# A two-layer S5, neighbourhood-attention and latent-attention block: the second layer's attention bias made in another stage, four gates moved to the first stage, the compressed projections cut in two jobs

## The chip, the cores and the metric

The kernel runs on one core of a Trainium2 chip. The metric is the device time of one execution in microseconds (us); lower is better. TensorE is PE in the rows (its weight loads PEld), VectorE is DVE, ScalarE is ACT, GpSimd is POOL, and SyncE, which here only issues transfers, is SP (SPq is its queue of transfers). Each engine, and each queue of transfers, runs its instructions in the order in which the program holds them.

## The reference

Two layers (`DEPTH = 2`) over 512 latent tokens (`x`) and 256 context tokens (`ctx`), 1024 channels, float32. Each layer feeds one modulated input `h` to three mixers and merges them:

```python
(ua, za, qn, kn, vn, zn, cq, ckv, kr, zm, ga, gn, gm) = split_cols(h @ w_in)
ya = s5_mixer(ua, ...)      # recurrence, then y = gelu(y); y * sigmoid(y @ w_glu + b_glu)
yn = neighbourhood_attention(qn, kn, vn, ..., rpb)     # bias from rpb, per layer
ym = block_attention(mla_queries(cq, ...), mla_keys_values(ckv, kr, ...))
m = (sig(ga) * ((ya * silu(za)) @ w_branch_a)
     + sig(gn) * ((yn * silu(zn)) @ w_branch_b)
     + sig(gm) * ((ym * silu(zm)) @ w_branch_c))
x = layer_norm(alpha * x + gate * (m @ w_out))
```

`cq`, `ckv` and `kr` are the compressed queries, keys and rotary keys (416 columns of `w_in`); `ga`, `gn` and `gm` are three gates of 1024 columns each; `rpb` is the table of the neighbourhood attention's bias. Only the latent tokens come out, so that the context's tokens go through the last half of layer 0 alone.

## The kernel before

Channels lie on the partitions and tokens along the free axis, 768 tokens (512 latent, 256 context). Every product is made in three passes: each operand is split into a rounded high part and the rest (`split`: ACT copies the high part, DVE or POOL subtracts), and PE multiplies high by high, low by high and high by low. A projection of 128 columns of `w_in` (`project`, matmuls at L232) is 24 matmuls of 512 tokens and 24 of 256 tokens; its weights are loaded as `wr` (four buffers), split into `wh` and `wl`. Low parts are `wl`, `hl`, `al` (line 145 on DVE or POOL), high parts `wh`, `hh`, `ah` (line 142 on ACT).

A layer has five stages, each with its own pools of SBUF. In the first (`s5a`) a string of letters, `JOBS[l]`, sets the order of the jobs: `u` makes the input of the recurrence, `a` and `m` the silu gates `za` and `zm` of two branches, `B` builds one of four sets of tables of the recurrence on DVE with small matmuls (L197, L659), `c` projects half of the compressed columns (three tiles of 128 tokens, matmuls at L1051), norms them, transposes them and stores them (`c_d`, `kr_d`), and `N` makes layer 0's bias table. Then come the neighbourhood attention and the recurrence (`na`), the latent attention (`mla`), the merge (`mrg`) and the output projection (`out`). In the profile layer 0's stages begin at about 0, 245, 478, 700 and 960 us, layer 1's at about 1085, 1200, 1390, 1570 and 1737.

The bias of layer `l` is made by `na_bias_layer`: for one or two heads three small loads from `rpb_d` fill 48 rows, POOL adds a mask, and one store writes `na_zd`. Layer 1's is made in layer 0's merge, in eight steps over four buffers of 480 columns.

The merge runs through branch b (8 blocks of 128 output channels), branch c (8 blocks, each with its gate `gm`), then the gates `ga` that are not yet made, then the S5 output's GLU (4 blocks of 24 matmuls), then branch a (8 blocks). `GX` says how many `ga` gates the latent attention makes in its spare room (two in layer 0, as gates 0 and 1; gates 2 to 7 are left to the merge). Work beside the blocks is placed by a string with a letter for each block:

```python
SIDE = ('T....B.B..N...G.........', '................G.......')
```

Position 0 is block 0 of branch b, position 8 block 0 of branch c: `T` and `B` make layer 1's tables, `N` its bias, `G` the gelu, which loads `y` (two buffers), squares, tanh on ACT, products on POOL and DVE, and splits into `ah0` and `al0`. All transfers of this stage go through SP's queue.

`split` goes round the engines by a counter: from the end of layer 0's first stage on, `flip` counts the calls and a table says for each stage which call in how many goes to DVE (`SE_REST = (3, (0,))`, one in three, holds in layer 1's merge).

## Time and profile before

| | |
|---|---|
| three runs | 1785.62, 1791.37, 1793.07 us (median 1791.37) |
| the profiled execution | 1788.85 us |
| its span, first to last instruction | 1787.1 us |
| mean granted clock of TensorE | 0.973 of full speed (2.4 GHz) |
| busy: PE, DVE, ACT, POOL | 1655.7, 1238.3, 746.9, 379.7 us |
| share of the span | 93%, 69%, 42%, 21% |

The span is 1.75 us shorter than the profiled execution's own time; a sum of changes of the span is made against 1788.85 us, which lies 2.52 us under the median. The busy shares are means over ten stages; what an edit is worth is read in its own stage.

### The profile page before, as it was taken

Reading aid. Unit: us, or ns where it says so; the run is one execution under the profiler, and the core shown is the slowest. Engines: PE = TensorE matmul, PEld = TensorE weight load, DVE = VectorE, ACT = ScalarE, POOL = GpSimd, SP = SyncE. Lnnn points to the kernel's source line nnn. Section 1 sums busy time; section 2 is a strip of 40 time slices with the busy share of each in tenths; the row PEclk is TensorE's granted clock in tenths of the full one; section 3 lists DMA queues with packets and bytes.
Section 4 is the critical chain, followed back from the end, with each engine's and each line's share of the span. In section 5 each row is a group of like instructions: output and inputs, shape, how many; then the busy total and the mean of one; then the engine's idle time right before and its main releaser. Section 6 shows DMA issues by size and latency. Waiting matters only on the chain.

```text
span 1787.1 us, 29011 instructions
## 1 busy us (share of the span) xinstructions
PE 1655.7 (93%) x10808; PEld 1387.4 (78%) x10808; DVE 1238.3 (69%) x2722; ACT 746.9 (42%) x1466; POOL 379.7 (21%) x284
## 2 busy tenths in 40 slices
PE   4899699999989999999799988899999999999996
PEld 2687588888878888878688767788888888788865
DVE  4899948877746564989357688838888666762257
ACT  4423344335355565222243345442344555642241
POOL 2000111012221101201403542001111311245382
PEclk9899799999999999999899999999999999999999
DMA  9567785345321122655756726755554422253462
GB/s 307 158 191 222 207 248 153 94 143 141 84 78 56 58 69 97 232 164 170 192 167 219 189 90 192 225 162 164 156 165 120 126 76 65 83 154 106 130 206 71
DMA packets 273076, 264.87 MB, mean 148 GB/s; under 512 B 70440, under 2 KB 227896, under 8 KB 272936
## 3 DMA queue, kind: packets, MB, share of 16 engines
q1 hardware_dynamic: 271736, 259.93, 49.4%
q0 software_dynamic: 1200, 3.10, 0.5%
q8 instruction: 85, 1.39, 0.3%
q14 instruction: 55, 0.45, 0.1%
HBM read 198.64 MB, written 68.53 MB: 149 GB/s over the span
## 4 chain that ended last, share of the span: by engine, by line
PE 59%; DVE 13%; DMA 6%; ACT 3%; issue 2%; POOL 2%; SPq 1%; DVEq 0%; ACTq 0%; POOLq 0%
PE g L232 35%; PE s L197 5%; PE w L1375 4%; PE s L1403 3%; PE g L1608 2%; DVE sb L145 2%; PE w L1174 2%; PE s L1213 2%; PE w L719 1%; DVE wl L145 1%; DVE ln_rs L148 1%; DMA y<-y_d 1%; DMA wr<-in_w_out 1%; POOL macc L145 1%; PE w L758 1%
## 5 line engine op out<-in xcount | busy, mean ns | idle before, releaser
L232 PE MATMUL g<-hh,wh 128*128 128x512 f32 (+1 forms) x1344 | 479.3, 358 | 16.3 <-ACT wh L142 11.9
L232 PE MATMUL g<-hl,wh 128*128 128x512 f32 (+1 forms) x1344 | 477.0, 355 | 2.7 <-POOL hl L145 1.5
L232 PE MATMUL g<-hh,wl 128*128 128x512 f32 (+1 forms) x1344 | 475.9, 355 | 1.1 <-DVE wl L145 1.1
L232 PEld LDWEIGHTS g<-hh,wh 128*128 128x128 f32 x1344 | 256.3, 191 | 55.9 <-ACT wh L142 12.8
L232 PEld LDWEIGHTS g<-hl,wh 128*128 128x128 f32 x1344 | 256.4, 191 | 37.7 <-DVE hl L148 2.5
L232 PEld LDWEIGHTS g<-hh,wl 128*128 128x128 f32 x1344 | 255.9, 190 | 36.9 <-DVE wl L145 2.8
L142 ACT ACTIVATE wh<-wr 128x1024 fp32r<-128x1024 f32 (+1 forms) x150 | 155.2, 1036 | 227.4 <-PE g L232 139.8
L145 DVE TENSOR_TENSOR wl<-wr,wh 128x1024 fp32r<-128x1024 f32 (+1 forms) x118 | 153.6, 1305 | 114.0 <-ACT wh L142 113.3
L232 PE MATMUL g<-al,wh 128*128 128x512 f32 (+1 forms) x336 | 120.4, 359 | 1.8 <-DVE al L145 1.8
L232 PE MATMUL g<-ah,wl 128*128 128x512 f32 (+1 forms) x336 | 118.7, 358 | 1.2 <-POOL wl L145 1.1
L232 PE MATMUL g<-ah,wh 128*128 128x512 f32 (+1 forms) x336 | 119.7, 361 | 0.0
L145 POOL TENSOR_TENSOR wl<-wr,wh 128x1024 fp32r<-128x1024 f32 (+1 forms) x32 | 74.9, 2339 | 201.7 <-ACT wh L142 183.9
L142 ACT ACTIVATE mla_pt<-s 128x384 f32<-128x384 f32 (+1 forms) x128 | 59.4, 475 | 86.5 <-PE s L197 85.9
L1377 DVE TENSOR_REDUCE mla_sm<-w 128x1 f32<-128x768 f32 (+1 forms) x80 | 67.9, 849 | 34.2 <-PE w L1375 33.3
L145 POOL TENSOR_TENSOR macc<-macc,g_t 128x768 f32<-128x768 f32 (+1 forms) x32 | 56.5, 1769 | 146.3 <-DVE g_t L148 146.3
L232 PEld LDWEIGHTS g<-ah,wh 128*128 128x128 f32 x336 | 63.4, 189 | 14.4 <-issue 3.1
L142 ACT ACTIVATE na_p<-w,na_sm 128x512 f32<-128x512 f32 (+1 forms) x80 | 50.8, 643 | 54.6 <-DVE na_sm L152 48.3
L232 PEld LDWEIGHTS g<-al,wh 128*128 128x128 f32 x336 | 63.9, 190 | 12.3 <-DVE al L145 2.5
L232 PEld LDWEIGHTS g<-ah,wl 128*128 128x128 f32 x336 | 63.9, 190 | 11.6 <-POOL wl L145 2.5
L1608 PE MATMUL g<-woh,hh 128*128 128x512 f32 (+1 forms) x168 | 64.9, 386 | 4.3 <-ACT woh L142 4.2
L142 ACT ACTIVATE mla_p<-w,mla_sm 128x768 f32<-128x768 f32 (+1 forms) x80 | 65.0, 813 | 4.7 <-DVE mla_sm L152 4.5
L1608 PE MATMUL g<-woh,hl 128*128 128x512 f32 (+1 forms) x168 | 64.5, 384 | 0.0
(350 smaller groups left out, 3417.5 us busy)
## 6 DMA issues: line engine op xcount, KB each, us to landing
wr<-in_w_in SPq DMA_DIRECT2D x104, 512.0 KB, 4.6
wr<-in_w_mod SPq DMA_DIRECT2D x32, 512.0 KB, 4.6
s_w<-s_w SPq DMA_DIRECT2D x32, 512.0 KB, 4.3
s_o<-s_o SPq DMA_DIRECT2D x16, 568.0 KB, 5.8
wr<-in_w_out SPq DMA_DIRECT2D x16, 512.0 KB, 3.6
s_o<-sb SPq DMA_DIRECT2D x12, 576.0 KB, 4.4
wr<-in_w_in SPq DMA_DIRECT2D x16, 416.0 KB, 4.6
s_rc<-s_r SPq DMA_DIRECT2D x16, 384.0 KB, 3.2
```

The costliest lines, as they stand in the source:

```text
L142: return S.activation(out=o, in_=i, func=f, **kw)
L145: return e.tensor_tensor(out=o, in0=x, in1=y, op=op)
L148: V.scalar_tensor_tensor(out=o, in0=x, scalar=s, in1=y, op0=op0, op1=op1)
L197: PE.transpose(o, i, ident[:n, :n])
L232: PE.matmul(o, w[:, k], x[:, k, 0:n], start=(k == 0 and i == 0), stop=(k == nk - 1 and i == 2))
L719: PE.matmul(pv[64 * e:64 * e + 64, r, g // 2], w[:, g, 64 * r:64 * r + 64], u[:, g, 32 * d:32 * d + 96], start=True, stop=True)
L1174: PE.matmul(q[:, e, c:c + 256], qs[:, e, cq], k_[:, e, w0:w0 + 256], start=(j == 0), stop=(j == 1))
L1213: PE.matmul(po[64 * e:64 * e + 64, 0:128], v_t[:, t, 64 * e:64 * e + 64], pt[:, e, n], start=(n == 0), stop=(n == len(kt) - 1))
L1375: PE.matmul(q[:, c], x[0:96, cq], y[0:96, c], start=(j == 0), stop=(j == 2))
L1377: V.tensor_reduce(out=sm[:, 3:4], in_=q[:, k0:TOK], axis=AX.X, op=ALU.max)
L1403: PE.matmul(po[64 * e_:64 * e_ + 64, 0:128], v_t[:, t, 128 * i + 64 * e_:128 * i + 64 * e_ + 64], p2[e_][:, n], start=(n == 0), stop=(n == ...
L1608: PE.matmul(o, x[:, k, tok], w[k][:, c], start=(k == 0 and i == 0), stop=(k == 7 and i == 2))
```

## The change

Three edits, in the tables of letters and in three functions.

First, layer 1's bias leaves the merge (the `N` of `SIDE[0]`) and is made in layer 0's latent attention: `na_bias_layer` becomes a generator, one step (three loads, one add, one store) each time it is advanced, over the two buffers `g_t` that the gates of that stage use. Second, a new job `g` makes four `ga` gates in layer 0's first stage, so the latent attention's two are gates 4 and 5 and the merge has gates 6 and 7 left. Third, `c` stops after the norm and POOL's copies; the transposes, roundings and stores of the half are a job `k` of their own. `G` keeps its position 14 in `SIDE[0]`; what stands between it and the GLU gets shorter by four gates.

```diff
-SIDE = ('T....B.B..N...G.........', '................G.......')
+SIDE = ('T....B.B......G.........', '................G.......')
-JOBS = ('uuBaBmaBmBacmaNmc', 'maaBmmaBcamucuuu')
+JOBS = ('uuBaBmaBmBgacgkmgaNcgmk', 'maaBmmaBcakmucuuku')
...
             tt(P, z, z, mk.unsqueeze(1).to_broadcast([48, 15 * nh, 32]), ALU.add)
             Q.dma_start(out=zd[:, h:h + nh], in_=z.rearrange("p (h r) c -> p h (r c)", h=nh))
-        return zd
+            yield
+        zds.append(zd)
...
+                    yield
                     for i in (3, 2, 0, 1):
...
+                def compress(half):
+                    started.append(compressed(half))
+                    next(started[-1])
+
+                def compress_end(half):
+                    next(started[half], None)
+
+                def gate_s5(b):
+
+                    z = T(sa, [128, TOK], "z", 2)
+                    for s, n, o in project(C_GA + 128 * b, need_ctx):
+                        act(z[:, s], o, AF.Tanh, scale=0.5)
+                    ga[b] = T(dr, [128, TOK], f"ga_d{l}{b}")
+                    Q.dma_start(out=ga[b][:, 0:n_tok], in_=z[:, 0:n_tok])
+                    mod_step()
...
+                bias = na_bias_layer(l + 1, pds[0], mp, "g_t", 2, 640) if need_ctx else iter(())
...
                     if i < 3:
                         gate_n(2 * i + 2)
+                        next(bias, None)
                         gate_n(2 * i + 3)
+                    for _ in range(2 if i < 3 else 9):
+                        next(bias, None)
                     for _ in range(GX[l][i]):
                         gate_s(len(ga))
...
-                def next_bias():
-                    zds.append(na_bias_layer(l + 1, pds[0], side["b"], "sb", SB[1], 480))
```

How the instructions move shows in three places. On PE, the end of layer 0's first stage before: the last matmuls of the second compressed half (L1051), and behind them at once the query projection of the next stage (`g_2703`).

```order
L1051 MATMUL s_2296<-wh_2371,hh1_610 128x416
L1051 MATMUL s_2296<-wl_2372,hh1_610 128x416
L1051 MATMUL s_2296<-wh_2371,hl1_611 128x416
L232 MATMUL g_2703<-hh0_608,wh_2699 128x512
L232 MATMUL g_2703<-hl0_609,wh_2699 128x512
L232 MATMUL g_2732<-hh1_610,wh_2699 128x256
```

The same end of the second compressed half in the change: a gate's projection follows (`g_2554`, the fourth of the new gates).

```order
L1054 MATMUL s_2417<-wh_2492,hh1_610 128x416
L1054 MATMUL s_2417<-wl_2493,hh1_610 128x416
L1054 MATMUL s_2417<-wh_2492,hl1_611 128x416
L232 MATMUL g_2554<-hh0_608,wh_2550 128x512
L232 MATMUL g_2554<-hl0_609,wh_2550 128x512
L232 MATMUL g_2580<-hh1_610,wh_2550 128x256
```

The query projection (`g_2947`) now stands behind that gate, the last `m` gate (`g_2642` is its second part) and the second half's transposes of `ct`.

```order
L232 MATMUL g_2642<-hl1_611,wh_2611 128x256
L232 MATMUL g_2642<-hh1_610,wl_2612 128x256
L197 MATMUL s_2670<-ident_60,ct_2514 64x128 x3
L197 MATMUL s_2681<-ident_60,ct_2514 128x128 x3
L197 MATMUL s_2688<-ident_60,ct_2514 128x128 x3
L197 MATMUL s_2695<-ident_60,ct_2514 128x128 x3
L232 MATMUL g_2947<-hh0_608,wh_2943 128x512
```

On SP, in layer 0's merge, before: the tail of the 24 bias loads and 8 stores, among them the weights of the gates (`wr`, L215), and then the gelu's loads of `y`.

```order
L361 DMA sb_9095<-rpb_d_2204 16x15x32 x2
L215 DMA wr_9714<-in_w_in 128x8x128
L363 DMA na_zd1_9052<-sb_9089 48x480
L1517 DMA ga_d02_9711<-g_t_9652 128x768
L215 DMA wr_9775<-in_w_in 128x8x128
L215 DMA wr_9836<-in_w_in 128x8x128
L363 DMA na_zd1_9052<-sb_9095 48x480
L215 DMA wr_9897<-in_w_in 128x8x128
L215 DMA wr_9958<-in_w_in 128x8x128
L1470 DMA y_9497<-y_d00_95 128x768
L1470 DMA y_9515<-y_d01_96 128x768
```

The same place in the change: the weights of the two gates that are left are issued ahead of the tables' last transfers (`s5_k11`, `s5_w111`, `s5_t11`), and `y` follows these directly.

```order
L215 DMA wr_9897<-in_w_in 128x8x128
L215 DMA wr_9958<-in_w_in 128x8x128
L684 DMA s5_k11_8920<-s5_kds_8951 128x2x240
L683 DMA s5_w111_8914<-s5_w_9020 128x1024
L687 DMA s5_t11_8919<-s5_k11_8920 128x1x128 x8
L1493 DMA y_9741<-y_d00_95 128x768
L1493 DMA y_9759<-y_d01_96 128x768
L215 DMA wr_10020<-in_ssm_w_glu 128x4x256
```

On POOL, in layer 0's latent attention before, the splits of weights (`wl`, `uql`) and of queries (`mla_ql`) follow each other.

```order
L145 TENSOR_TENSOR mla_ql_5578<-mla_q_5555,mla_qh_5577 96x768
L145 TENSOR_TENSOR wl_6455<-wr_6452,wh_6454 128x1024
L145 TENSOR_TENSOR wl_6515<-wr_6512,wh_6514 128x1024
L145 TENSOR_TENSOR mla_ql_6089<-mla_q_6066,mla_qh_6088 96x768
L145 TENSOR_TENSOR uql_6596<-uqr_6590,uqh_6595 128x512
L145 TENSOR_TENSOR wl_6988<-wr_6985,wh_6987 128x1024
```

In the change one addition of the bias (`g_t`, 48 rows of 480) stands between nearly any two of them.

```order
L145 TENSOR_TENSOR mla_ql_5822<-mla_q_5799,mla_qh_5821 96x768
L145 TENSOR_TENSOR g_t_6221<-g_t_6221,na_mk_6218 48x480
L145 TENSOR_TENSOR wl_6720<-wr_6717,wh_6719 128x1024
L145 TENSOR_TENSOR g_t_6287<-g_t_6287,na_mk_6218 48x480
L145 TENSOR_TENSOR wl_6786<-wr_6783,wh_6785 128x1024
L145 TENSOR_TENSOR g_t_6293<-g_t_6293,na_mk_6218 48x480
L145 TENSOR_TENSOR mla_ql_6354<-mla_q_6331,mla_qh_6353 96x768
L145 TENSOR_TENSOR uql_6879<-uqr_6873,uqh_6878 128x512
L145 TENSOR_TENSOR g_t_6776<-g_t_6776,na_mk_6218 48x480
```

One thing moves without being written. The counter of `split` starts at the end of the first stage; four gates fewer are split after it, so the calls of layer 1's merge fall one place further on in the cycle of three. At that merge's end, of the eight splits of the merged sum (`hl`) three were on DVE and five on POOL, and now two and six; of the four of the GLU's output (`al`) two were on DVE, and now none; of the last weight splits (`wl`) one more is on DVE.

## Rows read from the trace of the kernel before

**Rows 1.** The page's chain of work that ended last: shares of the span by engine.

```profile
PE 59%; DVE 13%; DMA 6%; ACT 3%; issue 2%; POOL 2%; SPq 1%; DVEq 0%; ACTq 0%; POOLq 0%
```

**Rows 2.** Windows, end of the first stage: us, busy (x instructions) by engine, PEclk, DMA.

```profile
200.00:210.00 10.00, 3.02 (x24) 2.16 (x24) 10.00 (x16) 1.41 (x2) 0.00 (x0) 0.50 0.63 199
210.00:220.00 10.00, 4.57 (x35) 3.90 (x36) 8.27 (x12) 3.81 (x9) 3.44 (x2) 0.58 0.96 230
```

**Rows 3.** PE's timeline, one projection's first matmul and the next one's: start, duration.

```profile
94.02 0.40 PE L232 MATMUL g<-hh,wh 128*128 128x512 f32 x1
...
102.36 0.40 PE L232 MATMUL g<-hh,wh 128*128 128x512 f32 x1
```

**Rows 4.** PE's timeline: last m gate's end, second compressed half, query projection's first matmul.

```profile
192.00 0.28 PE L232 MATMUL g<-hh,wl 128*128 128x256 f32 x1
...
219.70 0.46 PE L1051 MATMUL w<-wh,hh 128*128 128x416 f32 x1 [0.46 <-ACT s_w L142]
...
236.91 0.39 PE L232 MATMUL g<-hh,wh 128*128 128x512 f32 x1
```

**Rows 5.** The page's groups: DVE's split of a weight tile, busy us and mean ns.

```profile
L145 DVE TENSOR_TENSOR wl<-wr,wh 128x1024 fp32r<-128x1024 f32 (+1 forms) x118 | 153.6, 1305 | 114.0 <-ACT wh L142 113.3
```

**Rows 6.** Windows of layer 0's merge, columns as in rows 2.

```profile
870.00:880.00 10.00, 0.84 (x2) 0.75 (x3) 0.86 (x1) 1.06 (x1) 3.56 (x3) 0.69 0.76 193
```

**Rows 7.** SP's timeline in that merge: start, time on the queue, transfers.

```profile
848.01 1.39 SPq L361 DMA_DIRECT2D sb<-rpb_d  x3
...
856.68 5.07 SPq L686 DMA_DIRECT2D s_t<-s_k  x8
...
863.56 3.83 SPq L361 DMA_DIRECT2D sb<-rpb_d  x8
...
873.58 0.45 SPq L215 DMA_DIRECT2D wr<-in_w_in  x1
...
881.28 2.31 SPq L1470 DMA_DIRECT2D y<-y_d  x2
```

**Rows 8.** Timeline: the merge's gates, gelu's first and last step, GLU's first and last matmul.

```profile
860.51 0.50 PE L232 MATMUL g<-hh,wh 128*128 128x512 f32 x1
...
887.97 1.69 ACT L142 ACTIVATE y_t<-y 128x768 f32<-128x768 f32 x2 [5.55 <-DMA y<-y_d]
...
911.32 2.05 DVE L145 TENSOR_TENSOR al<-gf,ah 128x768 fp32r<-128x768 f32 x2
...
924.43 0.50 PE L232 MATMUL g<-ah,wh 128*128 128x512 f32 x1
...
943.49 0.28 PE L232 MATMUL g<-ah,wl 128*128 128x256 f32 x1
```

**Rows 9.** Windows of layer 0's latent attention, columns as in rows 2.

```profile
500.00:600.00 100.00, 94.44 (x653) 80.02 (x651) 56.54 (x122) 56.58 (x121) 20.42 (x11) 0.97 0.23 67
600.00:700.00 100.00, 98.17 (x778) 83.23 (x776) 59.02 (x154) 56.93 (x135) 8.59 (x5) 1.00 0.14 45
```

**Rows 10.** POOL's timeline there: a query split.

```profile
553.65 1.82 POOL L145 TENSOR_TENSOR mla_ql<-mla_q,mla_qh 96x768 fp32r<-96x768 f32 x1 [9.51 <-ACT mla_qh L142]
```

**Rows 11.** Bias of layer 1, tile view (ns min/median/max) and transfers (us to landing).

```profile
L361 SPq DMA_DIRECT2D sb<-rpb_d x24: 376/438/496, 848.0 to 873.1; - x24
L145 POOL TENSOR_TENSOR sb<-sb,na_mk x8: 1185/1214/1860, 852.2 to 875.2; 48x480 f32<-48x480 f32 x8
...
sb<-rpb_d SPq DMA_DIRECT2D x24, 30.0 KB, 2.2
```

**Rows 12.** Groups of 1690 to 1740 us: splits on POOL and on DVE.

```profile
L145 POOL TENSOR_TENSOR hl<-macc,hh 128x512 fp32r<-128x512 f32 x5 | 6.8, 1376 | 0.0
L145 POOL TENSOR_TENSOR al<-gf,ah 128x512 fp32r<-128x512 f32 x2 | 3.5, 1740 | 0.0
...
L145 DVE TENSOR_TENSOR hl<-macc,hh 128x512 fp32r<-128x512 f32 x3 | 3.7, 1243 | 7.3 <-ACT hh L142 7.3
L145 DVE TENSOR_TENSOR al<-gf,ah 128x512 fp32r<-128x512 f32 x2 | 2.8, 1386 | 1.4 <-ACT ah L142 1.4
```

More of the change, by code (lines that the diff above doesn't have):

```diff
@@ L877, in build @@
             u_d = []
+            ga = {}
             where[0] = f"s5a{l}"
@@ L1023, in biases @@
                     pds.append(na_bias_rows(sp))
-                    zds.append(na_bias_layer(0, pds[0], sa, "sb", SB[0], 960))
+                    for _ in na_bias_layer(0, pds[0], sa, "sb", SB[0], 960):
+                        pass
                 gq = T(sp, [128, 3], "mla_g")
@@ L1102, in compressed @@
                         Q.dma_start(out=kr_d[:, tok], in_=kpe)
-                jobs = {"u": input_s5, "a": gate_a, "m": gate_m, "c": compressed, "B": build_s5, "N": biases}
+                started = []
+                def compress(half):
[10 more added lines that the diff above has]
+                    mod_step()
+                jobs = {"u": input_s5, "a": gate_a, "m": gate_m, "c": compress, "k": compress_end, "g": gate_s5,
+                        "B": build_s5, "N": biases}
                 done = dict.fromkeys(jobs, 0)
@@ L1264, in build @@
             with phase("mla", 2, 2, 2, groups=G_MLA) as mp:
-                ga = {}
                 exps = {}
@@ L1492, in side_step @@
                         gelu()
-                    elif j in "TBN" and need_ctx:
-                        {"T": next_tables, "B": next_build, "N": next_bias}[j]()
+                    elif j in "TB" and need_ctx:
+                        {"T": next_tables, "B": next_build}[j]()
                 get = branch_w("w_branch_b")
```

## The prediction

> **What bounds the kernel now.** I read the chain of waits first. PE holds 59% of it, DVE 13%, the other engines and the transfers the rest [rows 1]. So what PE does, and where it stands idle, sets the time, and I went to the windows of the stages that the change touches to look for PE's idle time there.
>
> The first stage has a hole near its end: PE is busy 3.02 of the 10 us from 200 and 4.57 of the 10 from 210, while DVE is busy 10.00 and 8.27 with the recurrence's tables [rows 2]. The granted clock is 0.50 and 0.58 in these windows, near the lower level (1.2 of 2.4 GHz); before them PE had been idle. The last `m` gate ends on PE at 192.0, the second compressed half starts at 219.7 [rows 4]. Between them PE has only the tables' small matmuls, which wait for DVE. Work that is put there is nearly free.
>
> Layer 0's merge has a second hole: PE is busy 0.84 us from 870 to 880 [rows 6]. SP's timeline says why. Its queue issues the 24 bias loads from 848.0 to past 867, and a gate's weights, `wr`, come out only at 873.6; the gelu's first two loads of `y` come out at 881.3 [rows 7]. After that PE works on the gates without much waiting, until the GLU starts at 924.4 and ends at 943.5 [rows 8].
>
> The latent attention has no hole on PE: 94.4 of 100 us and 98.2 of 100 are busy, but POOL is busy only 20.4 and 8.6 of 100 and the transfer engines 0.23 and 0.14 [rows 9].
>
> **The change part by part.** *One gate.* A projection of 128 columns takes 102.36 - 94.02 = 8.34 us of PE [rows 3]. Four gates are 33.4 us, which leave the merge and enter the first stage; the total of PE's work stays.
>
> *First stage.* In the new order three of the four gates stand ahead of the second compressed half, and the last `m` gate goes behind it. So two projections more lie ahead, 16.7 us: PE would come to 192.0 + 16.7 = 208.7, still ahead of 219.7, where DVE and the compressed half's own inputs let it start. These 16.7 us are covered by the tables on DVE. Behind the second half now stand one new gate and the moved `m` gate, 16.7 us, before the query projection, which started at 236.9 [rows 4]. Nothing covers these: +16.7. The second half's transposes come ahead of the query projection rather than behind it, an exchange. DVE, which is full, gains three splits of gate weights ahead of the last tables and loses one, two at 1.31 us [rows 5]: 2.6 us at most, nothing if they fall into DVE's gaps of 1.73 us in the window from 210; I take 1.3. Sum +18. From below: if DVE gains nothing and a little of the 16.7 falls where the query projection had waited anyway, +14 (a quarter of one gate and the 1.3, an estimate). From above: nothing is covered, +33.4 (a rival). The cover is worth 16.7 us, which is what it costs if DVE finishes that much earlier or PE comes to the hole later.
>
> *The stores behind it.* On SP the loads of the recurrence's inputs for the next stage stand behind the second half's stores, which now come 18 us later. That costs nothing if the loads were early, and at most what a load took behind others, 887.97 - 881.28 = 6.7 us [rows 7, 8]; with it this stage's bounds are +14 and +24.
>
> *Merge.* Without the bias loads SP is free after the tables' last transfers, 856.68 + 5.07 = 861.75, and `y` follows them directly: 19.5 us earlier than 881.28 [rows 7]. The gelu took from the issue of `y` at 881.28 to its last low part, 911.32 + 2.05 = 913.37, that is 32.1 us [rows 8]. In the change it ends at 861.75 + 32.1 = 893.8. PE has, from 860.5 on, two gates, to 877.2, and then the GLU. The GLU took 943.5 - 924.4 = 19.1 us [rows 8]; a quarter of it, 4.8, is two blocks' products with the first half of the gelu's channels, which the new order puts ahead of the rest. So PE comes to 882.0, waits for the last low part until 893.8, and has 14.3 us left: 908.1 in place of 943.5, -35.4. The load of `y` was slow, the 6.7 us above from issue to use, and the chain ran beside five gates' work on ACT; each microsecond of it that falls away comes back. I take -37. From below, without any gain over the old pace and with 5 us lost to weights of branch a that now have to arrive sooner, -30; from above, no wait at all, the GLU straight behind the gates, 877.2 + 19.1 = 896.3, -47. So of the 33.4 + 9.2 us (four gates, and the hole of rows 6) that could go, some 6 to 12 go to the wait for the gelu, which is what is late next. PE will again stand idle for about ten microseconds; the old hole had a granted clock of 0.69 in its window [rows 6], and the price of that is in both.
>
> *Bias beside the latent attention.* Eight steps. One is three issues of 0.44 us, 2.2 us to landing, 1.21 us on POOL [rows 11] and the store, about 5 us of one chain and 9.7 us of POOL in all. PE waits for none of it unless a split stands behind it. POOL had 9.51 us idle ahead of a query split that took 1.82 [rows 10], and on SP the weights' loads of the next gate wait for a free buffer anyway. Only one gate buffer is left to the gates while the bias uses the other; a gate's store has to land before the next gate's first tanh, and between two gates lie the scores and values of several heads. I take +0.5, from 0 to +8 (three of the eight steps met by a split that waits half of the 5 us).
>
> *Layer 1's merge, by the counter.* At its end two `al` and one `hl` go from DVE to POOL and one `wl` back. By the rows, (1.74 - 1.39) x 2 + (1.38 - 1.24) = 0.8 us [rows 12], and POOL works there almost without pause, so it is paid; the `wl` that leaves gives some back, the last `al` comes somewhat later. I take +1, from -1 to +4. The Trainium skill (GPSIMD Engine Reference, section 4.1 Engine selection) puts GPSIMD at about half of VectorE's pace for elementwise work with two inputs. By that the three would cost 1.39 x 2 + 1.24 = 4.0 us more, and the sum would be 3 us later. This case's trace agrees for no pair in this stretch, 1376 against 1243 ns and 1740 against 1386 [rows 12].
>
> *Compressed halves in two jobs; gelu's place.* The first half's end comes later in the program, with DVE full anyway; layer 1's first stage keeps PE's order but for the transposes. The gelu keeps its position, so nothing of its own moves. 0, within 2 either way.
>
> **Sum.** 18 - 37 + 0.5 + 1 = -17.5 us. Against the profiled execution, 1788.85 - 17.5 = 1771.4. It lay 2.5 us under the median of the runs, so against the median the same sum gives 1773.9. I forecast 1772.
>
> **The rivals.**
>
> *The first stage takes all four gates at full price.* PE could come to the hole late: in the new order a gate stands ahead of the first compressed half, so the small matmuls that feed DVE come later too, and the tables end later by as much. Then +33.4 + 1.3 and the sum is -0.8: 1788 to 1790. For it: DVE is full, so each microsecond that its feeding matmuls come late is lost. Against it: these matmuls are placed between the gates' matmuls as before, and PE is idle 7.0 and 5.4 us in the two windows [rows 2]. Half way is -9.
>
> *The gelu stays as late as it was.* Nothing in the table moves it, and if the tables' last transfers or another wait hold `y` until about 881, it ends at 913.4 and the GLU cannot end before 913.4 + 14.3 = 927.7: -15.8, and the sum is +3.7: 1793. Against it: between these transfers and `y` SP's program holds nothing now.
>
> *On the other side: SP's queue in the latent attention.* SP issues in order; each step's store waits for POOL's addition, and POOL's addition may stand behind a split that waits for ACT. Behind the store stand the next gate's weights and the queries' weights. If PE has to wait out each step, 8 x 5 us = 40, the sum is +22: 1811 to 1813. It eats the gain at 17.5 / 8 = 2.2 us a step, and makes the kernel slower by over 0.5% at 3.3 us a step. For it: PE has no slack in this stage [rows 9], so every wait shows. Against it: POOL's and the transfers' shares [rows 9], and POOL's idle time ahead of its splits [rows 10].
>
> *More gain.* The gelu runs faster without the gates beside it and the GLU hardly waits: -47, sum -27.5: 1761 to 1764.
>
> **How the numbers follow.** 0.5% of 1791 is 9 us; less than that a measurement of this kernel can hardly tell from no change, so the border is 1782. The forecast has 0.70 (nearly all of it faster), the first stage at full price 0.12 (mostly no change), the late gelu 0.06 (no change), SP's queue 0.08 (slower), more gain 0.04 (faster). That gives faster 0.74, same 0.16, slower 0.10. The likeliest case alone runs from +14 - 47 to +24 - 30 + 8 + 4, at its likely ends 1758 to 1782; the range that leaves out 2 in 10 reaches into the full price of the first stage and leaves out SP's queue: 1757 to 1788.
>
> **What would show it.** In the first stage, PE busy 8 or more in the windows from 192 to 205, the second half still starting near 220, the query projection near 255. In the merge, no `rpb_d` loads on SP, `y` issued right behind `s_t`, PE idle once, between the second gate and the GLU's second half, for about 10 us, and the GLU ending about 19 us earlier on the clock of the whole span (-37 and the first stage's +18). In the latent attention, PE's busy share as before and POOL about 5 us more in each hundred. In layer 1's merge, one more `hl` on POOL. The forecast is wrong if the second half starts later than 225, if `y` does not follow `s_t` at once, or if the latent attention gets longer by more than 4 us.

## The result, and the profile after

The changed kernel takes 1765.4 us (median of four runs, 1759.7 to 1766.9) against 1788.5 for the kernel before beside it: a ratio of 0.987, with a 95% interval from 0.984 to 0.990. That is 23 us less, 1.3%. The forecast was 1772, with a range from 1757 to 1788.

The profiled execution took 1764.34 us, its span is 1762.5, the mean granted clock 0.984 (0.973 before). From the page, the busy times and the shares of the chain:

```profile
PE 1648.2 (94%) x10808; PEld 1380.7 (78%) x10808; DVE 1228.9 (70%) x2721; ACT 746.2 (42%) x1466; POOL 396.4 (22%) x285
...
PE 30%; DVE 8%; DMA 2%; issue 2%; ACT 2%; POOL 1%; SPq 1%; DVEq 0%; ACTq 0%; POOLq 0%
```

PE is busy 7.5 us less than before for the same products, 1655.7 - 1648.2. The chain's shares add up to less than half of the span here (46%, and 86% in [rows 1]), so they can't be compared; the stages can. The table takes the same PE instruction in two traces, by its start, and gives the changed kernel's time less that of before. Two of the experiments stand beside it.

| PE's instruction | before, us | change | bias alone | gates alone |
|---|---|---|---|---|
| first matmul of the second compressed half | 219.70 | +5.0 | -1.6 | +4.4 |
| neighbourhood attention, early (values) | 305.07 | +20.2 | -1.7 | +21.9 |
| the same, late (scores) | 477.97 | +17.5 | -1.7 | +19.2 |
| latent attention, early (scores) | 545.02 | +13.7 | -1.6 | +15.4 |
| first transpose behind it | 719.42 | +13.7 | -1.6 | +15.4 |
| merge, shortly before the gates | 865.43 | +14.1 | -1.5 | +18.4 |
| output projection, early | 982.14 | -27.4 | -13.1 | -0.7 |
| output projection, late | 1040.00 | -30.9 | -17.6 | -3.6 |
| layer 1's first stage | 1097.55 | -29.9 | -16.1 | -3.0 |
| layer 1's recurrence | 1209.45 | -25.3 | -12.4 | -3.1 |
| layer 1's latent attention, late | 1566.97 | -25.5 | -11.6 | -4.2 |
| last output projection | 1769.95 | -24.6 | -11.1 | -2.9 |

Two profiles of an unchanged stretch differ by up to some 4 us (the run with layer 1's compressed job in its old place, which edits nothing in layer 0, lies 2.9 to 3.8 us behind the changed kernel from layer 0's latent attention to its output projection), so that smaller steps of one column say nothing by themselves; a step is read together with a wait that the trace shows.

*First stage.* Windows of the changed kernel, columns as in [rows 2]:

```profile
200.00:210.00 10.00, 9.57 (x71) 8.31 (x69) 9.04 (x11) 4.38 (x10) 0.00 (x0) 1.00 0.45 113
210.00:220.00 10.00, 1.24 (x16) 0.86 (x8) 10.00 (x13) 1.64 (x3) 0.00 (x0) 0.82 0.82 267
```

PE's timeline there: the last matmul of the projections ahead of the second compressed half (an `a` gate, which stands behind the third new gate), the last table's matmuls, the second compressed half's first one, and the query projection's.

```profile
208.82 0.28 PE L232 MATMUL g<-hh,wl 128*128 128x256 f32 x1
...
220.10 1.08 PE L660 MATMUL s<-sb,s_b 128*32 128x128 f32 x16 [7.68 <-DVE sb L145]
...
224.68 0.46 PE L1054 MATMUL w<-wh,hh 128*128 128x416 f32 x1 [0.51 <-ACT s_w L142]
...
260.49 0.50 PE L232 MATMUL g<-hh,wh 128*128 128x512 f32 x1 [0.25 <-DVE z L148]
```

The gates fill the hole's first half, 9.57 of 10 us at a clock of 1.00 where [rows 2] had 3.02 at 0.50, and end at 209.1, as the prediction had it (208.7). But DVE ends the tables later and PE still waits 7.68 us for them, so the second half starts at 224.7 in place of 219.7 [rows 4].

DVE's timeline in the changed kernel says where it loses time:

```profile
199.38 0.28 DVE L335 COPY mod_g<-s 16x128 f32<-16x128 f32 x1 [2.14 <-PE s L197]
200.96 2.63 DVE L145 TENSOR_TENSOR sb<-s_c,s_p 128x1152 f32<-128x1152 f32 x2 [1.30 <-ACT s_c L142]
```

PE transposes `s_cn`, and ACT copies that to the `s_c` that DVE needs for the tables. PE's transposes, before and after:

```profile
194.84 0.44 PE L197 MATMUL s<-ident,s_cn 128*128 128x128 f32 x2
```

```profile
199.18 0.38 PE L197 MATMUL s<-ident,s_cn 128*128 128x128 f32 x2
```

They now come behind matmuls of the third gate. Until then DVE is not late: an operation on `s_kds` that started at 196.25 before starts at 195.79. The run with the gates alone has the same two waits (2.13 and 1.30 us), the run with the bias alone has neither.

*Merge.* Windows, columns as before:

```profile
870.00:880.00 10.00, 10.00 (x57) 8.02 (x56) 4.78 (x8) 1.33 (x2) 3.70 (x2) 1.00 0.59 173
880.00:890.00 10.00, 10.00 (x63) 9.01 (x62) 8.21 (x23) 5.99 (x9) 3.70 (x2) 1.00 0.93 318
890.00:900.00 10.00, 8.22 (x58) 5.57 (x56) 7.25 (x15) 6.00 (x9) 3.68 (x2) 1.00 0.72 244
900.00:910.00 10.00, 7.78 (x56) 5.21 (x57) 7.49 (x16) 5.18 (x8) 0.00 (x0) 1.00 0.71 227
```

The timeline, with SP's transfers, the gelu's first and last step, and the GLU's first matmul, its two longest waits and its last matmul:

```profile
863.51 1.01 SPq L215 DMA_DIRECT2D wr<-in_w_in  x2
...
871.46 5.05 SPq L687 DMA_DIRECT2D s_t<-s_k  x8
876.55 1.06 SPq L1493 DMA_DIRECT2D y<-y_d  x2
...
880.04 0.84 ACT L142 ACTIVATE y_t<-y 128x768 f32<-128x768 f32 x1 [4.88 <-DMA y<-y_d]
...
892.10 0.50 PE L232 MATMUL g<-ah,wh 128*128 128x512 f32 x1
...
900.60 0.97 PE L232 MATMUL g<-ah,wh 128*128 128x512 f32 x4 [1.42 <-ACT ah L142]
...
902.58 2.04 DVE L145 TENSOR_TENSOR al<-gf,ah 128x768 fp32r<-128x768 f32 x2
...
903.60 0.50 PE L232 MATMUL g<-al,wh 128*128 128x512 f32 x1 [1.04 <-DVE al L145]
...
917.44 0.28 PE L232 MATMUL g<-ah,wl 128*128 128x256 f32 x1
```

No bias load is left on SP and `y` goes out right behind `s_t`. The hole of [rows 6] is gone. PE's idle time at the GLU is 1.78 + 2.22 = 4.0 us, at a full clock; 1.42 + 1.04 = 2.5 of it is for the gelu's `ah` and `al`. The GLU's last matmul starts at 917.4, 26 us earlier than in [rows 8] although the merge began 14 later.

*Latent attention.* It is 174.4 us from the early score to the transpose behind it (545.02 to 719.42), and as long after (558.74 to 733.15). Two windows of 100 and 70 us in it before, and the same ones 14 us later after:

```profile
545.00:645.00 100.00, 99.60 (x726) 85.47 (x725) 55.05 (x128) 54.77 (x126) 10.98 (x6) 1.00 0.20 63
645.00:715.00 70.00, 68.25 (x560) 56.52 (x559) 41.60 (x119) 40.44 (x94) 9.17 (x5) 1.00 0.24 80
```

```profile
559.00:659.00 100.00, 99.66 (x727) 85.49 (x725) 56.07 (x130) 54.65 (x125) 18.19 (x12) 1.00 0.26 74
659.00:729.00 70.00, 68.27 (x559) 56.56 (x558) 41.20 (x119) 40.43 (x94) 9.18 (x5) 1.00 0.24 78
```

POOL has six operations and 7.2 us more in the first window, and PE does the same work in the same time.

### The profile page after: what moved, and what is told of

It is laid out like the page before. It is cut to its first block, busy times and chain, and to the rows that moved or that the text cites. A ratio compares the mean times of both kernels' runs of the same rounds, so it can differ in the third digit from the quotient of the medians.

```text
span 1762.5 us, 29023 instructions
## 1 busy us (share of the span) xinstructions
PE 1648.2 (94%) x10808; PEld 1380.7 (78%) x10808; DVE 1228.9 (70%) x2721; ACT 746.2 (42%) x1466; POOL 396.4 (22%) x285
## 5 line engine op out<-in xcount | busy, mean ns | idle before, releaser
L142 ACT ACTIVATE wh<-wr 128x1024 fp32r<-128x1024 f32 (+2 forms) x150 | 155.1, 1036 | 224.1 <-PE g L232 157.4
L145 POOL TENSOR_TENSOR macc<-macc,g_t 128x768 f32<-128x768 f32 (+1 forms) x32 | 63.6, 1992 | 137.6 <-DVE g_t L148 124.2
L232 PEld LDWEIGHTS g<-ah,wl 128*128 128x128 f32 x336 | 64.2, 191 | 12.9 <-DVE wl L145 2.4
L1081 POOL COPY ct<-ct 128x48 f32<-128x48 f32 x8 | 15.4, 1960 | 228.3 <-DVE ct L1069 228.3
```

Of the source, the lines that this page charges most:

```text
L142: return S.activation(out=o, in_=i, func=f, **kw)
L145: return e.tensor_tensor(out=o, in0=x, in1=y, op=op)
L232: PE.matmul(o, w[:, k], x[:, k, 0:n], start=(k == 0 and i == 0), stop=(k == nk - 1 and i == 2))
```

## Experiments

The kernel before took 1785.9, 1786.6, 1788.5 and 1786.2 us beside the four groups of runs; ratios are to these. What each run is set against is the changed kernel's 0.987 [0.984, 0.990], unless it says otherwise.

**The bias alone**: the kernel before with the bias in the latent attention, without job `g`.

```diff
-JOBS = ('uuBaBmaBmBgacgkmgaNcgmk', 'maaBmmaBcakmucuuku')
+JOBS = ('uuBaBmaBmBackmaNmck', 'maaBmmaBckamuckuuu')
```

> Only the bias moves into the latent attention; gates and compressed halves as before. Theory (each edit removes a wait that the other would leave): the latent attention keeps its length within 1 us; in the merge the hole of 9 us before the third gate goes and the gelu is done before the six gates are, so that the GLU ends some 14 us earlier: -14 us against before (-11 to -17). Rival A (the bias was the whole of the merge's gain): -30 or more, as in the full change less its first stage. Rival B (SP's queue in the latent attention pays for it): 0 or slower, with the latent attention longer by 5 us or more.

1776.9 us, 0.995 [0.993, 0.996]: 9 less than before. The table's column shows the latent attention unchanged and the merge 11.6 us shorter (-1.5 to -13.1), with PE busy in the stretch that had the hole:

```profile
870.00:880.00 10.00, 9.39 (x53) 7.91 (x53) 8.56 (x23) 5.71 (x9) 2.61 (x2) 1.00 0.79 243
880.00:890.00 10.00, 9.90 (x55) 8.37 (x54) 9.13 (x22) 6.14 (x9) 2.18 (x2) 1.00 0.40 128
```

So the bias is free in the new place, and leaving the merge is worth about the hole. The gain is 5 us smaller than expected and lies outside the range of -11 to -17: the merge gives 11.6 where 14 were expected, the output projection 4.5 that were not (-13.1 to -17.6), and layer 1's first stage takes 3.7 back (1097 to 1209).

**The gates alone**: the changed kernel with the bias back in the merge.

```diff
-SIDE = ('T....B.B......G.........', '................G.......')
+SIDE = ('T....B.B..N...G.........', '................G.......')
```

> Four gates in the first stage and the compressed halves in two jobs, the bias left in the merge. Theory: the first stage and what follows cost +14, the merge has two gates left but y is issued only after the bias, so that the GLU waits for the gelu and ends only some 16 us earlier than before on the merge's own clock; with +5 of layer 1 the sum is +3 us against before (-3 to +7). Rival A: the gates are worth what the full change gained less the bias's 14, that is -10.

1779.8 us, 0.997 [0.996, 0.998]: 6 less than before, where 3 more were expected (-3 to +7). The merge gave 3 us more than the theory had, and the 5 us that it put on layer 1 did not come. The profiled execution was the slowest of ten, 1786.1, so its column carries a few us too many. The merge is 19.1 us shorter, of 33.4 us of gates that left it. SP's timeline and one window of the merge say where the rest stayed:

```profile
880.85 4.29 SPq L361 DMA_DIRECT2D sb<-rpb_d  x8
...
897.57 2.27 SPq L1497 DMA_DIRECT2D y<-y_d  x2
```

```profile
890.00:900.00 10.00, 4.09 (x11) 3.31 (x12) 2.17 (x2) 2.11 (x2) 2.38 (x2) 0.50 0.92 294
```

The gates are gone, but the bias loads still hold `y` back to 897.6, and PE waits for the gelu at half the clock. The two edits give 9 and 6 us alone, and 23 together: the gates' removal pays only if what they covered, the gelu, comes earlier too.

**The bias twice**: the eight steps doubled, the second set into a tensor that nothing reads.

> The full change with the bias made twice in the latent attention (a second set of eight steps into a tensor that nobody reads), so 16 steps on SP, POOL and the same two buffers. Theory (the steps lie in idle time of SP and POOL and PE waits for none): the latent attention gets longer by 0 to 3 us, POOL's share rises by some 10 us. Rival (every step costs PE a part of its chain of 5 us, hidden so far by noise): +10 us or more.

One run: 1768.4 us, span 1766.6. The tile view of POOL's additions, with sixteen in place of eight:

```profile
L145 POOL TENSOR_TENSOR g_t<-g_t,na_mk x16: 1199/1214/1730, 538.3 to 651.6; 48x480 f32<-48x480 f32 x16
```

The latent attention grew by 1.8 us for eight steps more, where a step in the open would cost about 5 (over the same stretch the other runs with four gates agree within 0.1 us). The room for them is real. That PE begins to lose time at sixteen suggests that it ends near there, which one run does not settle.

**A gate ahead of the second half**: the fourth new gate moved into the hole.

```diff
-JOBS = ('uuBaBmaBmBgacgkmgaNcgmk', ...
+JOBS = ('uuBaBmaBmBgacgkmgagNcmk', ...
```

> The full change with the fourth new gate ahead of the second compressed half in place of behind it; PE stands idle for 7.7 us there, waiting for DVE's tables. Theory (the hole still has room for most of a projection of 8.3 us, DVE pays one more weight split of 1.3 us): -6 us against the full change (-4 to -8), about 1759. Rival (DVE is the bound there and every split or late matmul for it moves the end of the tables by as much): 0 to -2.

1760.0 us, 0.985 [0.983, 0.987]: 3 to 4 less than the changed kernel by the ratios, at the edge of what the intervals tell apart. PE is busy 9.66 us from 210 to 220 and the second half starts at 225.2 as before, but then there is a new wait. ACT's and PE's timeline:

```profile
234.34 0.58 ACT L142 ACTIVATE rms_c<-s,mla_g 128x384 f32<-128x384 f32 x1 [8.22 <-DMA c<-rms_c]
...
235.76 0.72 PE L1054 MATMUL w<-wh,hh 128*128 128x416 f32 x1 [3.11 <-ACT wh L142]
```

ACT waits until a store of the compressed half has landed and its buffer is free (two buffers of `rms_c`), the next weights' high parts are queued behind it, and PE waits for those. So the expected 6 us did not come in the first stage: the early values of the neighbourhood attention start at +20.1 in the table's way of counting (+20.2 in the changed kernel), the latent attention's early scores at +16.8 (+13.7). What this run gains lies in layer 1's first stage, which the edit does not touch: -27.2 at its start and -28.4 at its end, where the changed kernel has -29.9 and -25.3. What lies behind that is told at the end of the account.

**The same with four buffers** of `rms_c`:

> The kernel with the fourth gate ahead of the second compressed half, and four buffers in place of two for the rounded rows of the compressed halves (rms_c). In the run without them the hole was filled (PE 9.66 of 10 us from 210), yet ACT waited 8.2 us for a store of rms_c to land and PE 3.1 us for the weights behind it. Theory (that wait, not DVE, ate the gain): it goes, and the query projection starts 4 us earlier than in that run: -4 against it, about 1756 (-6.5 against the full change). Rival (DVE's tables or the second half's own chain set the end): the wait moves to another tile, 0 to -1 against it.

1758.8 us, 0.984 [0.983, 0.986]. ACT's wait for the store is gone. The query projection starts 3.2 us earlier than in the run above (255.0, 258.2), but its matmuls now take 0.63 us, where those of [rows 4] took 0.39 (the granted clock is 0.66 in the window from 250); PE's timeline:

```profile
254.98 0.79 PE L232 MATMUL g<-hh,wh 128*128 128x512 f32 x1
255.56 0.63 PE L232 MATMUL g<-hl,wh 128*128 128x512 f32 x1
```

The medians show 1.2 us of it, too little to tell from nothing. Still, this is the fastest kernel of the study: 0.984 against the changed kernel's 0.987, and 6 us below the run with the earlier gelu, which was measured beside it and equals the changed kernel. Most of that lies in layer 1's first stage again (-27.4 to -28.4, with the earlier gelu -27.4 to -24.2); at the early values of the neighbourhood attention it is 1.4 us ahead of the changed kernel (+18.8).

**The gelu two letters earlier**: `G` at position 12.

> The full change with the letter G really two positions up (12 in place of 14). Theory: y's tiles lie where the tables' working memory lay and its loads stand behind the tables' last transfers on SP's queue, so the letter moves nothing: 0 against the full change (-2 to +2), y still issued right behind s_t, the GLU's end on the merge's clock unchanged. Rival (the gelu's place in the program bounds it): y is issued 5 us or more earlier and the kernel gains the 4 us that PE still waits: -4.

1764.8 us, 0.988 [0.986, 0.989]: no difference. Its place in the string does not set when `y` can be loaded; `s_t` ahead of it does.

**Layer 1's compressed job in its old place**:

```diff
-JOBS = (..., 'maaBmmaBcakmucuuku')
+JOBS = (..., 'maaBmmaBckamuckuuu')
```

> The full change, but in layer 1 each compressed half is finished in one go as before (the job k right behind c). In the full change PE waits 4.17 us for the loads of s_w at the start of layer 1's neighbourhood stage, which before had no wait there. Theory: SP's order (the second half's stores, which wait for ACT, stand ahead of those loads) makes that wait; the kernel gets 4 us faster than the full change, about 1761. Rival (the shifted counter of splits or another load does it): the wait stays, 0.

1763.5 us, 0.987 [0.985, 0.988]: no difference. The theory that SP's order in layer 1's first stage cost 4 us is wrong; the wait for `s_w` stands in the kernel before as well, with 5.0 us.

**Three gates, and the last `m` gate ahead of the second half**:

```diff
-JOBS = ('uuBaBmaBmBgacgkmgaNcgmk', ...
+JOBS = ('uuBaBmaBmBgacgkmgamNck', ...
```

> Three gates in the first stage in place of four, all of them and the last m gate ahead of the second compressed half, so that nothing but its own end stands between it and the query projection; the merge then has three gates left. Theory: the first stage costs about 15 us less than in the full change (two projections that no hole covers, less the 2 us of the second half's own waits), the merge 8.3 us more less the 4 us that PE there waits for the gelu: -9 against the full change (-5 to -11), about 1755. Rival (the first stage's end is set by the second half's chain through ACT and the stores): -3 or less, as the one gate moved ahead gave.

1775.0 us, 0.994 [0.992, 0.995]: 10 more than the changed kernel, where 9 less were expected. Against the changed kernel's trace it has 11 of the expected 15 us at the end of the neighbourhood attention (-11.0) and loses them behind it: 9.6 in the first 60 us of the latent attention, 1.3 more up to the merge's gates, 5 by the middle of the output projection, and 6.5 behind that. The edit did more than it says. An odd number of gates left the stages behind the counter's start, so every later split that goes by two changed engines. The next three runs take that apart.

**The counter by itself**: the changed kernel, and behind layer 0's merge

```diff
+            if l == 0:
+                flip[0] += 1
             where[0] = f"out{l}"
```

> The changed kernel with one line more: behind layer 0's merge the split counter is advanced by 1, so that the output projection's and layer 1's latent attention's splits change places between DVE and POOL, and the cycle of three in layer 1's merge starts one further. Nothing of layer 0 moves up to there. Theory (the +6 to +7 us behind the merge in the run with three gates came from the counter): 1771 to 1773, and the trace longer from the output projection on. Rival (they came from the other places of layer 0's work): 1764 to 1767.

1773.1 us, 0.991 [0.989, 0.993]: 7.7 us lost by the medians, by a line that computes nothing. In the trace 5.4 of them (+0.9 at 1301, +6.4 at 1548) lie in and just ahead of layer 1's latent attention. The tile views of two splits there, the query's and the gates' weights', in the changed kernel:

```profile
L145 DVE TENSOR_TENSOR mla_ql<-mla_q,mla_qh x4: 677/682/689, 1403.1 to 1513.7; 96x512 fp32r<-96x512 f32 x4
L145 POOL TENSOR_TENSOR mla_ql<-mla_q,mla_qh x4: 1281/1395/1604, 1407.7 to 1519.2; 96x512 fp32r<-96x512 f32 x4
...
L145 DVE TENSOR_TENSOR wl<-wr,wh x7: 1220/1226/1227, 1384.7 to 1502.1; 128x1024 fp32r<-128x1024 f32 x7
```

and with the counter advanced:

```profile
L145 POOL TENSOR_TENSOR mla_ql<-mla_q,mla_qh x4: 1269/1319/1615, 1405.5 to 1520.4; 96x512 fp32r<-96x512 f32 x4
L145 DVE TENSOR_TENSOR mla_ql<-mla_q,mla_qh x4: 677/682/1786, 1411.2 to 1529.0; 96x512 fp32r<-96x512 f32 x4
...
L145 POOL TENSOR_TENSOR wl<-wr,wh x7: 2357/2379/2661, 1385.1 to 1508.1; 128x1024 fp32r<-128x1024 f32 x7
```

In each pair of queries the first now goes to POOL (1405.5) and takes 1.32 us in place of 0.68; and of the gates' weight splits in the stretch seven now take 2.38 us on POOL, where seven took 1.23 on DVE (others go the opposite way). That the line costs the time is shown; the way from these splits to PE is only argued, since PE waits for none of them directly. From 1380 to the end of the latent attention PE's waits grow from 4.6 to 8.6 us, the longest of them 2.8 for ACT's `g_t`, 1.2 for a key split and 1.2 for `mla_pt`, and the granted clock is 0.83 from 1520 to 1530, where the changed kernel has 1.00.

**Three gates with the counter put right** (`flip[0] += 5`):

> The run with three gates again, with the counter advanced by 5 behind layer 0's merge, so that all later splits lie on the engines where the changed kernel has them. Theory: 6 to 7 us less than with three gates, 1768 to 1769. Rival: 1775 as before.

1767.4 us, 0.989 [0.987, 0.991]: 7.6 us back, all of it behind the merge. Without the counter's part three gates in this order are 2 to 4 us behind four by the medians and ratios, which the intervals do not tell apart: the 11 us of the first stage go at the latent attention's start and in the merge, which has one gate more to do.

**The counter as before** (`flip[0] += 4`):

> The changed kernel with the counter advanced by 4 behind layer 0's merge: later splits lie where the kernel before has them. Theory (the term of +1 us for the counter's shift in layer 1's merge): 1 us less, 1764 to 1765, too little for the timing, and layer 1's merge 0.5 to 1.5 us shorter in the trace. Rival (the counter matters there as much as by parity): 5 us or more either way.

1763.7 us, 0.986 [0.984, 0.988]. Too little for the timing. From 1541 to 1727, layer 1's merge, the trace is 1.0 us shorter (-1.9 to -2.9), but the run with a gate ahead, whose splits there lie as in the changed kernel, is 2.1 shorter (-3.0 to -5.1), so this does not show the counter's part.

**The order of two splits in the kernel before.** The table's column falls from +17.5 to +13.7 at the latent attention's start. There the kernel before and the one with three gates have PE wait 3.4 us for keys, the changed one 1.2:

```profile
PE g L232 <- DVE mla_kl L145: 3.4, 1, 3.4
```

```profile
PE g L232 <- DVE mla_kl L145: 1.2, 1, 1.2
```

(before, and the changed kernel.) On DVE the build had put one split elsewhere, in the first the second line below, in the other the last:

```
mla_kl_5449<-g 64x512       mla_kl_5693<-g 64x512
mla_kl_5453<-mla_kp 32x768  mla_kl_5693<-g 64x256
mla_kl_5449<-g 64x256       mla_kl_5695<-g 64x512
mla_kl_5451<-g 64x512       mla_kl_5695<-g 64x256
mla_kl_5451<-g 64x256       mla_kl_5697<-mla_kp 32x768
```

```diff
                             tt(V, kk[e][1][0:64, s], oe, kk[e][0][0:64, s].bitcast(F32), ALU.subtract)
+                        if l == 0 and i == 0 and s.start == LAT:
+                            stt(kp[64:96, 0:1], o[64:96, 0:1], 0.0, kp[64:96, 0:1], ALU.mult, ALU.add)
```

> The kernel before with one small operation more at the start of layer 0's latent attention: behind the first pair's keys DVE adds zero times a column of their sum to a column of the rotary keys, so that the second pair's rotary keys have to be split behind the first pair's, as they are in the changed kernel, and not between its two parts. Theory (about 6 of the first stage's 20 us come back at the start of the latent attention because the build, whose scheduler settles the order there, puts this split elsewhere in the changed kernel): PE's wait of 3.4 us for the keys shrinks to 1.2 or less, its clock stays at 1.00, and the kernel takes 4 to 6.5 us less than before. Rival (the time comes back for another reason, such as the place of the last values of the neighbourhood attention): within 1.5 us of before.

1781.3 us against 1786.2, 0.997 [0.996, 0.999]: 4.9 less, inside what the theory gave, and yet the theory falls. PE's wait shrank to 2.0 us, but a wait of 1.2 for the query's split and a clock of 0.84 followed, and by 545 only 0.3 us of it were left. The time was won in the output projection (-1.5 at 982, -6.0 at 1040), which the edit doesn't touch. ACT's and PE's timeline there, in the kernel before:

```profile
997.92 1.06 ACT L142 ACTIVATE x<-x 128x1024 f32<-128x1024 f32 x1 [4.51 <-DMA x<-in_x]
1000.61 1.06 ACT L142 ACTIVATE x<-x 128x1024 f32<-128x1024 f32 x1 [1.63 <-DMA x<-in_x]
1001.81 1.06 ACT L142 ACTIVATE woh<-wr 128x1024 fp32r<-128x1024 f32 x1
...
1002.91 0.49 PE L1608 MATMUL g<-woh,hh 128*128 128x512 f32 x1 [2.75 <-ACT woh L142]
```

and ACT's in this run:

```profile
994.35 1.06 ACT L142 ACTIVATE x<-x 128x1024 f32<-128x1024 f32 x1 [2.45 <-DMA x<-in_x]
996.21 1.06 ACT L142 ACTIVATE x<-x 128x1024 f32<-128x1024 f32 x1 [0.80 <-DMA x<-in_x]
997.37 1.06 ACT L142 ACTIVATE woh<-wr 128x1024 fp32r<-128x1024 f32 x1
```

In the kernel before the last weights of the output projection are split behind two scalings that wait for `x`, PE waits for them and goes on at a lower clock (0.83 in the window from 1000). With `x` 2 us earlier from issue to landing (10.9 in place of 12.9) PE does not wait. Why it lands earlier is open, with one trace of each. The changed kernel does not have this wait either.

## Why the prediction was right, step by step

**The whole**: -23.1 us by the medians and -24.5 between the two profiled executions (1764.34 - 1788.85), where the sum said -17.5. The measured time lies in the likely case, and no rival took its place: the second half did not take four gates at full price, `y` came early, and the latent attention did not wait for SP's queue. But the rival of more gain (1761 to 1764) lies nearer to the measured time than the forecast does, and the merge went about half way to it.

**First stage, +18 forecast.** +20.2 at its consequences in the neighbourhood attention; at the query projection it is +23.6 (260.5, where the prediction named 255), and the second half's transposes now stand ahead of that. The two uncovered projections are in it as priced, and PE has no wait for the loads behind the second half's stores. The mis-sized term is DVE's, put at +1.3, with 2.6 at most, for splits of gate weights. The last tables' matmuls come 5.1 us later (214.97 to 220.10), 4.0 of it behind 192, and in this stretch DVE has no split of a gate's weights. It has one split of compressed weights (1.0 us) and one product of a gate (0.7) more, and it stands idle 3.1 us in place of 0.8, which is the two waits for PE's transposes and ACT's `s_c`. So a few microseconds came by the mechanism of the first rival, small matmuls that reach DVE late because a gate stands ahead of them. The prediction held against it that they are placed as before; PE's transposes of `s_cn` come 4.3 us later. The second half started at 224.7, near the 225 that the prediction named as its limit.

**What came back at the latent attention's start, -6.5, was not forecast.** At 497.7, the last values of the neighbourhood attention, the delay is still +19.4; by 545 it is +13.7, and with the gates alone it falls as much (+21.9 to +15.4). From 495 to 540 PE waits 3.3 us in the changed kernel, 5.3 in the kernel before, and its clock stays at 1.00, where the kernel before has 0.93 and 0.73 in the windows from 500 and 510. It does not go with four gates as such: with the fourth gate ahead of the second half PE waits 5.0 us there, its clock falls to 0.86, and the delay at 545 is +16.8. The key split's place was tried and gives 0.3 us. Which difference of order at that border decides is open. That the time lies below the forecast is so in part luck: without these 6.5 us the change would have given 18, close to the sum.

**Merge, -37 forecast.** -41.5 (+14.1 to -27.4), within the bounds. By its parts: `y` was issued at 876.6, where 861.75 + 14.1 gives 875.9; the GLU started at 892.1, where 877.2 + 14.1 gives 891.3. The mis-sized term is PE's wait for the gelu, put at 6 to 12 us: PE stood idle 4.0 us there, 2.5 of it for the gelu. The gelu took 28.1 us (876.55 to 904.62) in place of 32.1. Of these 4 us 3.2 are the load of `y`, from issue to the first step 3.5 us (876.55 to 880.04) in place of 6.7. The chain behind the load took 24.6 us in place of 25.4, and 24.4 in the run with the bias alone, where the gates still ran beside it; the gates' work on ACT, which the prediction named beside the load, had not slowed it. And a third of the GLU's matmuls (33 of 96), with 24 matmuls of the modulation, stood ahead of its last low part, where the prediction had a quarter. The runs agree with this account: bias alone -11.6, less 33.4 for four gates, plus some 4 of new idle time, is -41.

**Bias in the latent attention, +0.5 forecast.** 0.0 by two profiles, and the doubled bias shows that it is cover and not chance. The rival on SP's queue, 40 us, is out.

**Layer 1's merge, +1 forecast.** +0.9 in the profiles (last two lines of the table), and 1.0 less when the counter is put back. But over the same two lines the other runs whose splits lie as in the changed kernel give -1.2 to +1.3, so that the size of the term is not shown. It was small, and that was luck in one respect: four is even. The prediction followed the counter by three alone; an odd number of gates would have moved the splits that go by two, which costs some 8 us.

**Not forecast at all**: -3.5 in layer 0's output projection, where the kernel before waits for `x` (every run's trace gains there, 2.9 to 4.9 us, whatever its edit), and +4.6 in layer 1's first stage (-29.9 to -25.3), which some runs show and some don't. The trace shows an order on ACT behind it; ACT's timeline in the changed kernel, and in the kernel before:

```profile
1139.60 0.58 ACT L142 ACTIVATE rms_c<-s,mla_g 128x384 f32<-128x384 f32 x1 [6.14 <-DMA c<-rms_c]
1140.08 1.05 ACT L142 ACTIVATE wh<-wr 128x1024 fp32r<-128x1024 f32 x1
```

```profile
1165.08 1.06 ACT L142 ACTIVATE wh<-wr 128x1024 fp32r<-128x1024 f32 x1 [2.88 <-PE s L1051]
1168.68 0.58 ACT L142 ACTIVATE rms_c<-s,mla_g 128x384 f32<-128x384 f32 x1 [2.54 <-DMA c<-rms_c]
```

It is the wait for a store of `rms_c` that the run with a gate ahead has in layer 0. Where the build puts the third `rms_c` ahead of the next weights' high part, PE waits for the latter, 2.3 us in the changed kernel; where it stands behind, or has four buffers, PE does not. All seven runs with the first order have PE's wait (2.0 to 2.5 us) and take 27.1 to 29.1 us over one stretch of PE's program (1118.6 to 1146.6 in the changed kernel, 1147.9 to 1171.1 in the kernel before); the four with the other order and the one with four buffers take 23.2 to 24.2. (The two runs in which an odd count moved the splits have another order on PE there.) No edit goes with this order, so that it is chance of the build, and by the traces the two fastest kernels of the study owe their lead over the changed one to it. The two parts nearly cancel, so they did not help the total.

## What to carry to other kernels

Ask of each piece of work that is moved what it covered: here the gates hid a late gelu, and taking them away paid in full only with the transfer that made it late. A counter that deals work round the engines is an edit to every later stage; when the number of calls changes, follow it by each modulus that is in use, or start it anew at each stage. And read where a gain lies before it is credited: one run gained what was forecast, and two became the fastest, in stages that they had not touched.

## What the runs showed of the hardware

POOL took 2379 ns for the 128x1024 split for which DVE took 1226, and 1395 against 682 for 96x512, ratios of 1.9 and 2.0. The Trainium skill (GPSIMD Engine Reference, section 4.1 Engine selection) puts two-input elementwise work on GPSIMD at about half of VectorE's pace, and these rows agree. The pairs of [rows 12], on which the prediction set the rule aside, are the exception: there DVE took 1243 ns for 128x512, not less than for twice the columns above. The same split on DVE takes 694 ns as the median of the kernel before's eleven. Why these three are slower no run here shows; in the stretch DVE is busy 27.3 of 50 us and POOL 38.6.
